# Two recurrent mixers of a decoder layer: post stages taken in turn, and 64-row products issued in pairs

## The chip, the cores and the metric

The kernel runs on one core of a Trainium2 chip. The metric is the device time of one execution in microseconds. The kernel before was timed three times; the median is 2287.77 us (2284.74 to 2293.57).

## The reference

Two decoder layers work on 512 tokens of width 1024 in float32. Each layer adds three sub-layers to x, each between two RMS norms:

```python
ff = swiglu(rms_norm(x, g0), w1, w3, w2);  x = x + 0.5 * rms_norm(ff, g1)      # FFN A, 1024 -> 2816 -> 1024
p  = rms_norm(x, g2) @ w_in                                                    # one projection for three mixers
y_a = rwkv7_time_mix(...)    # 4 heads x 64, delta-rule state, scan over tokens
y_b = s5_mix(...)            # complex diagonal state space
y_c = gated_deltanet_mix(...)# 4 heads x 128, chunked delta rule
x = x + rms_norm(concat(y_a, y_b, y_c) @ w_out, g3)
ff = swiglu(rms_norm(x, g4), ...);         x = x + 0.5 * rms_norm(ff, g5)      # FFN B
```

RWKV's step is `S = S*w + (S nkk) b + v k` and `y = S r` for every token. GDN carries a state from chunk to chunk in the same manner. Both are computed here in chunks of 128 tokens: products inside a chunk give triangular matrices, which are inverted, and then the state goes through the chunks one after the other.

## The kernel before

The 512 tokens are two halves of 256; a half is two chunks (c = 0, 1) of 128. The program is a list of stages, a letter, the layer and the half: `A00 a01 P00 M00 A01 o00 P01 r01 O00 g01 M01 B00 O01 ...`, and the same for layer 1, which ends `g11 M11 B10 O11 b10 B11`. A and B are the FFNs, P the projection, M the mixers, O the output projection. A stage M has much small work, and so the FFN of the other half is written behind it: A01 behind M00, B00 behind M01, A11 behind M10, B10 behind M11. Instructions that are written earlier have the higher rank, and a planner with a cost model sets each engine's order when the program is built. On the chip each engine keeps that order and waits where an operand isn't there yet.

All weights are float32. ScalarE splits each tile into a rounded high part (`whi`, line 226) and VectorE makes the low part (`wlo`, line 227); a product is three matmuls (lines 245 to 247), named `ph` (FFN up), `acc` (FFN down and output projection), `pp` and `pg`. The small products of the mixers are plain float32 matmuls, each of which the trace shows as two instructions.

RWKV's chunk products (lines 754 to 777, in `rwkv`). The four heads lie in pairs j = 0, 1 on 128 partitions; a head of 64 rows is the lower (o = 0) or the upper half (o = 1) of them. For each chunk c and each o, two products over 64 rows (j = 0, 1) go to a PSUM tile `pk` (line 760), VectorE masks it into `AK` (line 761); two more go to a PSUM tile `pb` (line 764), and VectorE makes `AT` (line 767, twice) and `AB` (line 769) of it. Behind both o stand the products `pav` (line 774) and their copies `RV` and `YV`. `mx` is the PSUM tag of all the mixers' small products; it has two buffers of one bank each.

The post stages (`rwkv_post`, line 780; `gdn_post`, line 962) carry the states. `mix` calls rwkv_post(0), gdn_post(0), rwkv_post(1), gdn_post(1). Each is a chain in which TensorE and VectorE (with ScalarE and GpSimd at the norms) take turns: rwkv_post from line 791 to the copy into `mixT` at line 852; gdn_post from line 976 to the copy at line 1033. `mixT` is what stage O multiplies by w_out (lines 1349 to 1356). GDN's SBUF tiles and many others share the tag `b2` with 12 buffers, RWKV's have the tag `b1` with 7.

Of the kernel before, what the change touches and what calls it, by code (L numbers as in the profile page):

```python
# [16 lines left out]
AF = mybir.ActivationFunctionType  # L17
ALU = mybir.AluOpType
AX = mybir.AxisListType

P = 128
# [20 lines left out]
class Trunk:  # L42
# [601 lines left out]
    def rwkv(self, l, h, I):  # L644
        nc, L = self.nc, self.L
# [45 lines left out]
        be = self.b2([P, 2, 2, P], "be")  # L691
# [50 lines left out]
        for src, dst, sc in ((be, bn, -1.0), (ka, kn, 1.0), (vv, vn, 1.0)):  # L742
            pt = self.mx([P, 2, 2, P], "ptn")
            m = 2 if h == 0 or src is vv else 1
            for c in range(m):
                for j in range(2):
                    nc.tensor.transpose(pt[:, c, j], src[:, j, c], self.ident)
            nc.scalar.activation(dst[:, 0:m].rearrange("p c (j k) -> p c j k", j=2), pt[:, 0:m], AF.Copy, scale=sc)

        AT = self.b4([P, 8, P], "AT")  # L750
        AB = self.b4([P, 8, P], "AB")
# [1 line left out]
        YV = self.b2([P, 2, 256], "YV")  # L753
        for c in range(2):
            AK = self.b4([P, 2, 2, 2, P], "AK")
            for o in range(2):
                q = slice(64 * o, 64 * o + 64)
                pk = self.mx([P, 2, 2, P], "pk")
                for j in range(2):
                    nc.tensor.matmul(pk[:, j], ka[q, j, c], ar[q, j, c], start=True, stop=True)  # L760
                nc.vector.tensor_tensor(AK[:, :, o], pk, self.maskK.unsqueeze(1).to_broadcast([P, 2, 2, P]), ALU.mult)
                pb = self.mx([P, 2, 2, P], "pb")
                for j in range(2):
                    nc.tensor.matmul(pb[:, j], be[q, j, c], ar[q, j, c], start=True, stop=True)
                for j in range(2):
                    hd = 2 * j + o
                    nc.vector.scalar_tensor_tensor(AT[:, 4 * c + hd], pb[:, j, 0], rn2[:, c, hd:hd + 1], self.maskB[:, 0],
                                                   ALU.mult, ALU.mult)
                nc.vector.tensor_tensor(AB[:, 4 * c:4 * c + 4].rearrange("p (j o) t -> p j o t", o=2)[:, :, o], pb[:, :, 1],
                                        self.maskB[:, 1:2].to_broadcast([P, 2, P]), ALU.mult)  # L770
            pv = self.mx([P, 2, 256], "pav")
            for z in range(2):
                for hd in range(4):
                    nc.tensor.matmul(pv[:, z, 64 * hd:64 * hd + 64], AK[:, hd // 2, hd % 2, z], vn[:, c, 64 * hd:64 * hd + 64],
                                     start=True, stop=True)
            nc.vector.tensor_copy(RV[:, c], pv[:, 0])
            nc.scalar.activation(YV[:, c], pv[:, 1], AF.Copy)
        yield dict(AT=AT, AB=AB, ar=ar, RV=RV, YV=YV, kn=kn, bn=bn, vn=vn, rn2=rn2, sb=sb, gref=gref, gend=gend, sg=sg)

    def rwkv_post(self, l, h, c, R_, W, mixT):  # L780
# [4 lines left out]
        if not first:  # L785
            S0 = self.b1([P, 2, P], "S0")
            for j in range(2):
                nc.vector.tensor_scalar(S0[:, j], self.Sr[:, j], gref[:, j, c:c + 1], None, ALU.mult)
            p1 = self.mx([P, 256], "p1")
            for j in range(2):  # L790
                nc.tensor.matmul(p1[:, j * P:(j + 1) * P], ar[:, j, c, 0], S0[:, j], start=True, stop=True)
            R = self.b1([P, 256], "R")
            nc.vector.tensor_tensor(R, p1, RV[:, c], ALU.add)
        else:
            R = RV[:, c]
        p2 = self.mx([P, 256], "p2")
        for hd in range(4):
            nc.tensor.matmul(p2[:, 64 * hd:64 * hd + 64], W[:, 4 * c + hd], R[:, 64 * hd:64 * hd + 64], start=True, stop=True)
        SA = self.b1([P, 256], "SA")
        nc.vector.tensor_tensor(SA.rearrange("p (h k) -> p h k", h=4), p2.rearrange("p (h k) -> p h k", h=4),  # L800
                                rn2[:, c].unsqueeze(2).to_broadcast([P, 4, 64]), ALU.mult)
        if not last:
            p3 = self.mx([P, 2, P], "p3")
            for j in range(2):
                s = slice(j * P, (j + 1) * P)
                nc.tensor.matmul(p3[:, j], kn[:, c, s], vn[:, c, s], start=True, stop=False)
                nc.tensor.matmul(p3[:, j], bn[:, c, s], SA[:, s], start=False, stop=True)
            Sn = self.lay.tile([P, 2, P], F32, tag="Sr", name=self.n("Sr"), bufs=2)
            if first:
                t = p3  # L810
            else:
                t = self.b1([P, 2, P], "St")
                nc.vector.tensor_tensor(t, p3, S0, ALU.add)
            bdm = self.hmask
            for j in range(2):
                nc.vector.scalar_tensor_tensor(Sn[:, j], t[:, j], gend[:, j, c:c + 1], bdm, ALU.mult, ALU.mult)
            self.Sr = Sn
        p4 = self.mx([P, 256], "p4")
        for j in range(2):
            if not first:  # L820
# [4 lines left out]
                                 start=first, stop=first or o == 1)  # L825
        y = self.b1([P, 4, 64], "y")
        nc.vector.tensor_tensor(y, p4.rearrange("p (h k) -> p h k", h=4), YV[:, c].rearrange("p (h k) -> p h k", h=4), ALU.add)

        bc = lambda t: t.unsqueeze(2).to_broadcast([P, 4, 64])
        s1 = self.sm([P, 4], "gs1")  # L830
# [15 lines left out]
        pg = self.mx([P, 256], "pg")  # L846
        nc.tensor.matmul(pg, sg[:, c * P:(c + 1) * P], L["wg2"], start=True, stop=True)
        nc.vector.tensor_tensor(yf, yf, pg, ALU.mult)
        pt = self.mx([P, 2, P], "pty")
        for j in range(2):  # L850
            nc.tensor.transpose(pt[:, j], yf[:, j * P:(j + 1) * P], self.ident)
# [111 lines left out]
    def gdn_post(self, l, h, c, I, G_, W, mixT):  # L963
# [9 lines left out]
        for src, dst, sc in ((lambda hd: v2[:, hd, tk], vs, sk), (lambda hd: qk[:, hd, 0, tk], kd, kds))[:1 if last else 2]:  # L973
            pt = self.mx([P, 4, P], "ptg")
            for hd in range(4):
                nc.tensor.transpose(pt[:, hd], src(hd), self.ident)
            nc.vector.tensor_tensor(dst, pt, bch(sc[:, h4]), ALU.mult)
        if not first:
            S = self.Sg
            p1 = self.mx([P, 4, P], "g1")  # L980
            for hd in range(4):
                nc.tensor.matmul(p1[:, hd], qk[:, hd, 0, tk], S[:, hd], start=True, stop=True)
            R = self.b2([P, 4, P], "Rg")
            for hd in range(4):
                nc.vector.scalar_tensor_tensor(R[:, hd], p1[:, hd], neg[:, 4 * c + hd:4 * c + hd + 1], vs[:, hd],
                                               ALU.mult, ALU.add)
            if not last:
                Sd = self.b2([P, 4, P], "Sd")
                nc.vector.tensor_tensor(Sd, S, bch(eg[:, 1, h4]), ALU.mult)
        else:  # L990
            R = vs
        p2 = self.mx([P, 4, P], "g2")
# [1 line left out]
            nc.tensor.matmul(p2[:, hd], W[:, 4 * c + hd], R[:, hd], start=True, stop=True)  # L994
        vt = self.b2([P, 4, P], "vt")
        nc.vector.tensor_tensor(vt, p2, bch(es[:, h4]), ALU.mult)
        if not last:
            p5 = self.mx([P, 4, P], "g5")
            for hd in range(4):
                nc.tensor.matmul(p5[:, hd], kd[:, hd], vt[:, hd], start=True, stop=True)  # L1000
            Sn = self.lay.tile([P, 4, P], F32, tag="Sg", name=self.n("Sg"), bufs=2)
            if first:
                nc.scalar.activation(Sn, p5, AF.Copy)
            else:
                nc.vector.tensor_tensor(Sn, p5, Sd, ALU.add)
        o = self.b2([P, 4, P], "og")
        if not first:
            p3 = self.mx([P, 4, P], "g3")
            for hd in range(4):
                nc.tensor.matmul(p3[:, hd], qk[:, hd, 1, tk], S[:, hd], start=True, stop=True)  # L1010
            nc.vector.tensor_tensor(o, p3, bch(eg[:, 0, h4]), ALU.mult)
        p4 = self.mx([P, 4, P], "g4")
        for hd in range(4):
            nc.tensor.matmul(p4[:, hd], AQ[:, 4 * c + hd], vt[:, hd], start=True, stop=True)
# [1 line left out]
            nc.scalar.activation(o, p4, AF.Copy)  # L1016
        else:
            nc.vector.tensor_tensor(o, p4, o, ALU.add)
        if not last:
            self.Sg = Sn  # L1020
        osq = self.b2([P, 4, P], "osq")
        ss = self.sm([P, 4], "oss")
        for hd in range(4):
# [3 lines left out]
        nc.gpsimd.tensor_tensor(r, r, rqs[:, h4], ALU.mult)  # L1027
        for hd in range(4):
            nc.vector.scalar_tensor_tensor(o[:, hd], o[:, hd], r[:, hd:hd + 1], gw[:, c, hd * P:(hd + 1) * P], ALU.mult, ALU.mult)
        pt = self.mx([P, 4, P], "pto")  # L1030
        for hd in range(4):
            nc.tensor.transpose(pt[:, hd], o[:, hd], self.ident)
# [286 lines left out]
    def mix(self, l, h, I):  # L1319
        mixT = self.inp.tile([P, KT, HALF], F32, tag="mixT", name=self.n("mixT"))  # L1320
        if "R" not in I:
            I["R"] = self.rwkv(l, h, I)
            next(I["R"])
        R_ = next(I["R"])
        G_ = self.gdn(l, h, I)
        ATs = (R_["AT"], G_["AT"])
        X0 = self.inverse(ATs)
        self.s5(l, h, I, mixT)
        W = self.inverse2(ATs, X0)
        for c in range(2):  # L1330
            self.rwkv_post(l, h, c, R_, W[0], mixT)
            self.gdn_post(l, h, c, I, G_, W[1], mixT)
        return mixT

    def outmul(self, l, k, mixT, plain, chunks, accs):
# [153 lines left out]
```

## Time and profile before

| | us |
|---|---|
| median of three runs | 2287.77 |
| the profiled execution | 2288.75 |
| its span in the profile | 2287.0 |
| TensorE busy (15800 matmul instructions) | 2226.2, 97% |
| VectorE busy | 1688.1, 74% |
| ScalarE busy | 1192.6, 52% |
| GpSimd busy | 168.2, 7% |
| granted TensorE clock, mean | 0.989 |

Times in the rows below are us from the start of the span; "x" ahead of a number is a count. Matmuls overlap in the array, and so what one costs is read from start to start, not from its duration.

### The profile page before, as it was taken

The page shows a single profiled execution, that of the slowest core. Times are in us where ns is not written, and L with a number is a line of the kernel's source. Part 1 is how long each engine was busy: PE and PEld are TensorE (multiplying, and loading weights), DVE is VectorE, ACT ScalarE, POOL GpSimd, SP SyncE. Part 2 cuts the span into 40 slices and gives each one's busy share as a digit, 9 for nine tenths or more (in the row PEclk, how much of TensorE's full clock was granted, in tenths as well). Part 3 has the DMA queues.
Part 4 walks back from the last instruction along what each step waited for, and adds up shares of the span by engine and source line. Part 5 has one row for each costly group of instructions (what it writes and reads, how often), then busy time and mean ns, then how long its engine had stood idle before and what let it go on. Part 6 is the DMA issues. An engine that isn't in the chain of part 4 may idle for free. (4 is left out here: it accounts for less than half of the span.)

```text
span 2287.0 us, 44455 instructions
## 1 busy us (share of the span) xinstructions
PE 2226.2 (97%) x15800; PEld 2043.2 (89%) x15800; DVE 1688.1 (74%) x3771; ACT 1192.6 (52%) x2521; POOL 168.2 (7%) x372
## 2 busy tenths in 40 slices
PE   8998999999999999999999999999999999998998
PEld 7998999997979999799899999889987889987997
DVE  6697886966877866859776688687687678667665
ACT  5555754544645544545555567445455445445554
POOL 2032000001100001202200010000020000001000
PEclk9999999999999999999999999999999899999999
DMA  6676764645765645576666677456467366445665
GB/s 200 197 210 189 182 189 138 202 141 175 192 184 169 188 137 151 172 204 205 205 178 188 187 195 193 140 181 176 141 192 217 105 184 170 137 137 179 190 187 156
DMA packets 604963, 403.67 MB, mean 177 GB/s; under 512 B 63306, under 2 KB 534340, under 8 KB 604740
## 3 DMA queue, kind: packets, MB, share of 16 engines
q1 hardware_dynamic: 604740, 400.82, 60.7%
q8 instruction: 124, 2.03, 0.4%
q14 instruction: 99, 0.81, 0.1%
HBM read 387.09 MB, written 13.63 MB: 175 GB/s over the span
## 5 line engine op out<-in xcount | busy, mean ns | idle before, releaser
L226 ACT ACTIVATE whi<-raw 128x512 fp32r<-128x512 f32 (+2 forms) x1296 | 813.0, 632 | 848.2 <-PE ph L246 418.6
L227 DVE TENSOR_TENSOR wlo<-raw,whi 128x512 fp32r<-128x512 f32 (+2 forms) x1296 | 888.6, 690 | 419.1 <-ACT whi L226 403.9
L247 PE MATMUL ph<-hth,wlo 128*128 128x256 f32 x2464 | 704.7, 286 | 5.2 <-DVE wlo L227 5.2
L245 PE MATMUL ph<-hth,whi 128*128 128x256 f32 x2464 | 701.3, 285 | 6.6 <-DVE gu L364 3.4
L246 PE MATMUL ph<-htl,whi 128*128 128x256 f32 x2464 | 701.9, 285 | 3.3 <-DVE htl L318 3.0
L245 PEld LDWEIGHTS ph<-hth,whi 128*128 128x128 f32 x2464 | 467.7, 190 | 19.4 <-issue 3.9
L246 PEld LDWEIGHTS ph<-htl,whi 128*128 128x128 f32 x2464 | 466.9, 190 | 16.5 <-DVE htl L318 4.5
L247 PEld LDWEIGHTS ph<-hth,wlo 128*128 128x128 f32 x2464 | 467.5, 190 | 13.8 <-DVE wlo L227 8.6
L246 PE MATMUL acc<-wlo,gh 128*128 128x512 f32 x704 | 276.2, 397 | 0.0
L247 PE MATMUL acc<-whi,gl 128*128 128x512 f32 x704 | 270.3, 396 | 0.0
L245 PE MATMUL acc<-whi,gh 128*128 128x512 f32 x704 | 256.8, 400 | 0.7 <-ACT whi L226 0.7
L247 PEld LDWEIGHTS acc<-whi,gl 128*128 128x128 f32 x704 | 131.4, 188 | 28.5 <-issue 0.3
L246 PEld LDWEIGHTS acc<-wlo,gh 128*128 128x128 f32 x704 | 131.9, 188 | 23.2 <-issue 1.0
L245 PEld LDWEIGHTS acc<-whi,gh 128*128 128x128 f32 x704 | 130.2, 189 | 23.1 <-issue 1.4
L245 PE MATMUL pp<-hth,whi 128*128 128x256 f32 x352 | 99.1, 282 | 1.7 <-ACT whi L226 1.6
L245 PE MATMUL ph<-hx,whi 128*128 128x256 f32 x352 | 99.7, 283 | 0.9 <-DVE gu L364 0.9
L370 ACT ACTIVATE gh<-gu 128x256 fp32r<-128x256 f32 x176 | 71.7, 408 | 53.5 <-DVE gu L364 52.3
L246 PE MATMUL ph<-hx,whi 128*128 128x256 f32 x352 | 99.5, 283 | 0.0
L247 PE MATMUL ph<-hx,wlo 128*128 128x256 f32 x352 | 99.4, 282 | 0.0
L247 PE MATMUL pp<-hth,wlo 128*128 128x256 f32 x352 | 98.6, 282 | 0.5 <-DVE wlo L227 0.5
L246 PE MATMUL pp<-htl,whi 128*128 128x256 f32 x352 | 98.7, 282 | 0.0
L245 PE MATMUL pp<-hx,whi 128*128 128x256 f32 x352 | 98.6, 281 | 0.0
(491 smaller groups left out, 3391.8 us busy)
## 6 DMA issues: line engine op xcount, KB each, us to landing
raw<-in_ffn_w SPq DMA_DIRECT2D x1056, 256.0 KB
raw<-in_w_in SPq DMA_DIRECT2D x176, 256.0 KB
raw<-in_w_out SPq DMA_DIRECT2D x96, 256.0 KB
raw<-in_w_in SPq DMA_DIRECT2D x32, 260.0 KB
gain<-in_norm_gain SPq DMA_DIRECT2D x28, 256.0 KB
lx<-s5w SPq DMA_DIRECT2D x16, 384.0 KB
lv<-s5w SPq DMA_DIRECT2D x16, 256.0 KB
x<-in_x SPq DMA_DIRECT2D x4, 512.0 KB
```

Of the source, the lines that this page charges most:

```text
L226: nc.scalar.activation(hi, q, AF.Copy)
L227: nc.vector.tensor_tensor(lo, q, hi.bitcast(F32), ALU.subtract)
L245: mm(out, lh, rh, start=start, stop=False)
L246: mm(out, lh, rl, start=False, stop=False)
L247: mm(out, ll, rh, start=False, stop=stop)
L370: nc.scalar.activation(gh, u, AF.Copy, scale=0.5)
```

## The change

The four products of the two `pk` tiles of a chunk are issued as one sequence that alternates between upper and lower rows (o = 1, 0), one PSUM tile for each half; then the same for the two `pb` tiles. The first product of such a pair waits for what frees both tiles (`behind`), the others are kept in order by `after`, which adds no wait. For `pb` that is the second `AK` operation and a new one-column VectorE copy, `seen`, that reads its result. The post stages become generators that stop at `yield`; `mix` takes them in turn. When one says True, its state is done, and the same mixer's chunk 1 is put at the head of the list.

```diff
-            nc.scalar.activation(dst[:, 0:m]..., pt[:, 0:m], AF.Copy, scale=sc)
+            freed = [nc.scalar.activation(dst[:, 0:m]..., pt[:, 0:m], AF.Copy, scale=sc)]
...
         for c in range(2):
             AK = self.b4([P, 2, 2, 2, P], "AK")
+            def pair(name, a, behind):
+                ps = [self.mx([P, 2, 2, P], name) for _ in range(2)]
+                i = None
+                for j in range(2):
+                    for o in (1, 0):
+                        q = slice(64 * o, 64 * o + 64)
+                        m = nc.tensor.matmul(ps[o][:, j], a[q, j, c], ar[q, j, c], start=True, stop=True)
+                        if i is not None:
+                            self.after(m, i)
+                        else:
+                            for b in behind:
+                                self.tc.add_manual_dep(m.ins, b.ins.name, mybir.DependencyInfo(
+                                    mybir.DependencyClass.Sync, mybir.DependencyReason.SCHED_ONLY), reason="pair")
+                        i = m
+                return ps
+            pks = pair("pk", ka, freed)
             for o in range(2):
-                q = slice(64 * o, 64 * o + 64)
-                pk = self.mx([P, 2, 2, P], "pk")
-                for j in range(2):
-                    nc.tensor.matmul(pk[:, j], ka[q, j, c], ar[q, j, c], start=True, stop=True)
-                nc.vector.tensor_tensor(AK[:, :, o], pk, self.maskK..., ALU.mult)
-                pb = self.mx([P, 2, 2, P], "pb")
-                for j in range(2):
-                    nc.tensor.matmul(pb[:, j], be[q, j, c], ar[q, j, c], start=True, stop=True)
+                kept = nc.vector.tensor_tensor(AK[:, :, o], pks[o], self.maskK..., ALU.mult)
+            pbs = pair("pb", be, [kept, nc.vector.tensor_copy(self.sm([P, 1], "seen"), AK[:, 1, 1, 1, P - 1:])])
+            for o in range(2):
+                pb = pbs[o]
                 for j in range(2):          # AT and AB as before
...
-            nc.vector.tensor_copy(RV[:, c], pv[:, 0])
-            nc.scalar.activation(YV[:, c], pv[:, 1], AF.Copy)
+            freed = [nc.vector.tensor_copy(RV[:, c], pv[:, 0]), nc.scalar.activation(YV[:, c], pv[:, 1], AF.Copy)]
...
# rwkv_post: "yield" after R, SA, y and the gate product; "yield True" after the new state Sr
# gdn_post:  "yield" after each of vs and kd, R, vt, the first og, the second og, the normed og;
#            "yield True" after the new state Sg (self.Sg = Sn moves up there)
...
-        for c in range(2):
-            self.rwkv_post(l, h, c, R_, W[0], mixT)
-            self.gdn_post(l, h, c, I, G_, W[1], mixT)
+        live = [(self.rwkv_post(l, h, 0, R_, W[0], mixT), 0), (self.gdn_post(l, h, 0, I, G_, W[1], mixT), 1)]
+        while live:
+            for t in list(live):
+                said = next(t[0], False)
+                if said is False:
+                    live.remove(t)
+                elif said and t[1] < 2:
+                    live.insert(0, (self.gdn_post(l, h, 1, ...) if t[1] else self.rwkv_post(l, h, 1, ...), 2))
```

## Rows read from the trace of the kernel before

**Rows 1.** The page: engine, busy us, share of the span, instructions.
```profile
PE 2226.2 (97%) x15800; PEld 2043.2 (89%) x15800; DVE 1688.1 (74%) x3771; ACT 1192.6 (52%) x2521; POOL 168.2 (7%) x372
```
**Rows 2.** Waits of PE: line waited for, us in total, times, longest.
```profile
PE pto L1032 <- DVE og L1029: 2.5, 2, 2.0
```
**Rows 3.** Stage of the chunk products in M00: stretch, length, busy us by engine, PEclk, DMA share, GB/s.
```profile
326.80:360.80 34.00, 34.00 (x214) 28.31 (x212) 22.27 (x54) 12.48 (x24) 0.00 (x0) 1.00 0.44 129
```
**Rows 4.** Timeline of PE, stage M00: start us, us, instruction.
```profile
336.57 0.28 PE L245 MATMUL ph<-hth,whi 128*128 128x256 f32 x1
336.79 1.13 PE L764 MATMUL pb<-ar,be 64*128 64x256 f32 x4
337.84 0.39 PE L246 MATMUL ph<-htl,whi 128*128 128x256 f32 x1
338.07 0.28 PE L247 MATMUL ph<-hth,wlo 128*128 128x256 f32 x1
338.19 0.28 PE L245 MATMUL ph<-hth,whi 128*128 128x256 f32 x1
```
**Rows 5.** Timeline of PE, stage M01, where two groups lie together.
```profile
678.42 0.28 PE L245 MATMUL ph<-hth,whi 128*128 128x256 f32 x1
678.62 0.48 PE L764 MATMUL pb<-ar,be 64*128 64x256 f32 x1
678.64 0.48 PE L760 MATMUL pk<-ar,ka 64*128 64x256 f32 x1
...
679.39 0.38 PE L760 MATMUL pk<-ar,ka 64*128 64x256 f32 x1
679.70 0.39 PE L246 MATMUL ph<-htl,whi 128*128 128x256 f32 x1
679.92 0.28 PE L247 MATMUL ph<-hth,wlo 128*128 128x256 f32 x1
```
**Rows 6.** Timeline of PE, stage M11.
```profile
1793.67 0.41 PE L245 MATMUL ph<-hth,whi 128*128 128x256 f32 x1
1794.01 2.07 PE L764 MATMUL pb<-ar,be 64*128 64x256 f32 x4
1796.02 0.58 PE L246 MATMUL ph<-htl,whi 128*128 128x256 f32 x1
1796.39 0.41 PE L247 MATMUL ph<-hth,wlo 128*128 128x256 f32 x1
```
**Rows 7.** Stretches of stage M11, columns as in rows 3.
```profile
1789.50:1806.60 17.10, 17.10 (x54) 12.56 (x54) 8.37 (x28) 4.01 (x8) 0.00 (x0) 0.50 0.06 16
2051.03:2055.76 4.73, 4.73 (x11) 3.76 (x12) 2.34 (x5) 2.10 (x4) 0.00 (x0) 0.50 0.49 154
```
**Rows 8.** Instructions on tile pk: duration ns min/median/max, first and last start.
```profile
L760 PE MATMUL pk<-ar,ka x64: 376/376/792, 333.4 to 1814.1; 64*128 64x256 f32 x64
L761 DVE TENSOR_TENSOR AK<-pk,maskK x16: 678/692/694, 334.6 to 1814.5; 128x512 f32<-128x512 f32 x16
```
**Rows 9.** Instructions on tile pb.
```profile
L764 PE MATMUL pb<-ar,be x64: 376/376/792, 336.8 to 1817.3; 64*128 64x256 f32 x64
L767 DVE SCALAR_TENSOR_TENSOR AT<-pb,rn,maskB x32: 335/343/351, 338.0 to 1818.0; 128x128 f32<-128x128 f32 x32
L769 DVE TENSOR_TENSOR AB<-pb,maskB x16: 406/412/416, 338.5 to 1818.3; 128x256 f32<-128x256 f32 x16
```
**Rows 10.** Timeline of PE, first product of M11's post stages.
```profile
1959.57 0.61 PE L791 MATMUL p<-S,ar 128*128 128x128 f32 x4
```
**Rows 11.** Instructions on tile mixT between 1950 and 2052 us.
```profile
L852 ACT ACTIVATE mixT<-pty x2: 384/384/385, 1983.6 to 2030.7; 128x256 f32<-128x256 f32 x2
L1033 ACT ACTIVATE mixT<-pto x2: 597/598/599, 2009.8 to 2050.4; 128x512 f32<-128x512 f32 x2
```
**Rows 12.** Timeline of PE at the end of M11's post stages.
```profile
2047.71 0.30 PE L1032 MATMUL pto<-ident,og 128*128 128x128 f32 x1 [2.00 <-DVE og L1029]
2051.03 0.79 PE L245 MATMUL acc<-whi,mh 128*128 128x512 f32 x1 [0.69 <-ACT mixT L1033]
```

More of the change, by code (lines that the diff above doesn't have):

```diff
@@ L747, in rwkv @@
                     nc.tensor.transpose(pt[:, c, j], src[:, j, c], self.ident)
-            nc.scalar.activation(dst[:, 0:m].rearrange("p c (j k) -> p c j k", j=2), pt[:, 0:m], AF.Copy, scale=sc)
+            freed = [nc.scalar.activation(dst[:, 0:m].rearrange("p c (j k) -> p c j k", j=2), pt[:, 0:m], AF.Copy, scale=sc)]
         AT = self.b4([P, 8, P], "AT")
@@ L755, in rwkv @@
             AK = self.b4([P, 2, 2, 2, P], "AK")
-            for o in range(2):
-                q = slice(64 * o, 64 * o + 64)
-                pk = self.mx([P, 2, 2, P], "pk")
-                for j in range(2):
-                    nc.tensor.matmul(pk[:, j], ka[q, j, c], ar[q, j, c], start=True, stop=True)
-                nc.vector.tensor_tensor(AK[:, :, o], pk, self.maskK.unsqueeze(1).to_broadcast([P, 2, 2, P]), ALU.mult)
-                pb = self.mx([P, 2, 2, P], "pb")
-                for j in range(2):
-                    nc.tensor.matmul(pb[:, j], be[q, j, c], ar[q, j, c], start=True, stop=True)
+            def pair(name, a, behind):
[14 more added lines that the diff above has]
+            pks = pair("pk", ka, freed)
+            for o in range(2):
+                kept = nc.vector.tensor_tensor(AK[:, :, o], pks[o], self.maskK.unsqueeze(1).to_broadcast([P, 2, 2, P]), ALU.mult)
+            pbs = pair("pb", be, [kept, nc.vector.tensor_copy(self.sm([P, 1], "seen"), AK[:, 1, 1, 1, P - 1:])])
+            for o in range(2):
+                pb = pbs[o]
                 for j in range(2):
@@ L793, in rwkv_post @@
             nc.vector.tensor_tensor(R, p1, RV[:, c], ALU.add)
+            yield
         else:
@@ L801, in rwkv_post @@
                                 rn2[:, c].unsqueeze(2).to_broadcast([P, 4, 64]), ALU.mult)
+        yield
         if not last:
@@ L817, in rwkv_post @@
             self.Sr = Sn
+        yield True
         p4 = self.mx([P, 256], "p4")
@@ L827, in rwkv_post @@
         nc.vector.tensor_tensor(y, p4.rearrange("p (h k) -> p h k", h=4), YV[:, c].rearrange("p (h k) -> p h k", h=4), ALU.add)
+        yield
         bc = lambda t: t.unsqueeze(2).to_broadcast([P, 4, 64])
@@ L848, in rwkv_post @@
         nc.vector.tensor_tensor(yf, yf, pg, ALU.mult)
+        yield
         pt = self.mx([P, 2, P], "pty")
@@ L977, in gdn_post @@
             nc.vector.tensor_tensor(dst, pt, bch(sc[:, h4]), ALU.mult)
+            yield
         if not first:
@@ L989, in gdn_post @@
                 nc.vector.tensor_tensor(Sd, S, bch(eg[:, 1, h4]), ALU.mult)
+            yield
         else:
@@ L996, in gdn_post @@
         nc.vector.tensor_tensor(vt, p2, bch(es[:, h4]), ALU.mult)
+        yield
         if not last:
@@ L1005, in gdn_post @@
                 nc.vector.tensor_tensor(Sn, p5, Sd, ALU.add)
+            self.Sg = Sn
+        yield True
         o = self.b2([P, 4, P], "og")
@@ L1011, in gdn_post @@
             nc.vector.tensor_tensor(o, p3, bch(eg[:, 0, h4]), ALU.mult)
+            yield
         p4 = self.mx([P, 4, P], "g4")
@@ L1018, in gdn_post @@
             nc.vector.tensor_tensor(o, p4, o, ALU.add)
-        if not last:
-            self.Sg = Sn
+        yield
         osq = self.b2([P, 4, P], "osq")
@@ L1029, in gdn_post @@
             nc.vector.scalar_tensor_tensor(o[:, hd], o[:, hd], r[:, hd:hd + 1], gw[:, c, hd * P:(hd + 1) * P], ALU.mult, ALU.mult)
+        yield
         pt = self.mx([P, 4, P], "pto")
@@ L1329, in mix @@
         W = self.inverse2(ATs, X0)
-        for c in range(2):
-            self.rwkv_post(l, h, c, R_, W[0], mixT)
-            self.gdn_post(l, h, c, I, G_, W[1], mixT)
+        live = [(self.rwkv_post(l, h, 0, R_, W[0], mixT), 0), (self.gdn_post(l, h, 0, I, G_, W[1], mixT), 1)]
[5 more added lines that the diff above has]
+                elif said and t[1] < 2:
+                    live.insert(0, (self.gdn_post(l, h, 1, I, G_, W[1], mixT) if t[1] else self.rwkv_post(l, h, 1, R_, W[0], mixT), 2))
         return mixT
```

## The prediction

> **What bounds the kernel now.** I read the page's table of engines first: TensorE is busy for 2226.2 of 2287.0 us, VectorE for 1688.1, ScalarE for 1192.6 [rows 1]. Then the list of TensorE's waits: at the post stages it has one line, the last transposes `pto` behind VectorE's `og`, twice, 2.5 us in all [rows 2]; no line there has a wait on `AK`, `AT` or `AB`. Then the stretches in which the chunk products run: in M00 TensorE is busy for all of 34.00 us, VectorE for 22.27, the DMA engines for 0.44 [rows 3]. So in these stages TensorE's order is full, the FFN of the other half lies between the small products, and an instruction that goes there is time that the stage gives back. Last the timeline around single products, since busy time hides what overlaps: a full FFN matmul `ph` starts 0.12 us behind the one before it, although it lasts 0.28 [rows 4].
>
> **Change 1, the 64-row products.** In each of the four stages M there are 2 chunks x 2 halves x 2 kinds = 8 groups, 32 in all; a group is two products, four instructions (64 + 64 instructions on `pk` and `pb` in the trace [rows 8, 9]). The price of a group is read from start to start over its neighbours: from 336.57 to 338.07 is 1.50 us, in which two `ph` steps of 0.12 stand, so 1.26 us: 1.05 for the four instructions, 0.20 for going from `ph` to them and back [rows 4].
>
> What two groups cost when they lie together the trace before already shows once. In M01 a `pb` group of the lower rows met a `pk` group of the upper rows: their instructions start 0.02 us apart (678.62 and 678.64), all eight have started by 679.39, and from 678.42 to 679.92 is again 1.50 us [rows 5]. So eight instructions on both halves cost the same 1.26 us as four on one. That is the pattern that the change makes on purpose, with two PSUM tiles as there.
>
> The clock was not the same in all stages. From 1789.50 to 1806.60 the granted clock was 0.50 of full speed, which is 1.2 GHz [rows 7]; a group there costs 1796.39 - 1793.67 = 2.72 us less two `ph` steps of 0.215, so 2.29 us [rows 6]. Four of M11's groups fall into it, the other 28 run at 2.4 GHz, two of these together. Before: 27 x 1.26 + 4 x 2.29 = 43.2 us. After, 16 pairs: 14 x 1.26 + 2 x 2.29 = 22.2 us. TensorE saves 21.0 us.
>
> Bounds: if the halves did not overlap, a pair would cost 2 x 1.05 + 0.20 = 2.30 instead of 2.52, and 16 x 0.2 = 3 us would be left (the change of neighbours alone). If each change between lower and upper rows cost as much as one half of the way from `ph` and back, 0.10, three such changes in a pair take 16 x 0.3 = 5 us, and 2 us would be lost. So 2 us lost to 21.0 saved; I take 21.0, because the row nearest to it is the same two instructions on the same operands [rows 5]. It goes to the end undiminished: TensorE is full there [rows 3], and what it finds earlier is the FFN that would run next.
>
> **What the pairs add.** The first product of a pair now waits for both tiles, and everything behind it on TensorE's order waits too. For `pb` that is two `AK` operations of 0.692 us and the copy `seen` (its price has no row; nothing to 0.34, the time of an `AT` operation on 128 columns, and I take a little over half) [rows 8, 9]: 1.4 to 1.7 us of VectorE that have to be filled with some 12 to 15 `ph` matmuls of 0.12. Before, every group waited in the same way for a tile that VectorE or ScalarE frees, and the order kept them apart: 3.4 us lie between the first `pk` (333.4 [rows 8]) and the first `pb` (336.8 [rows 9]), filled with `ph` (the last of them stands in [rows 4]), and TensorE did not wait. I expect the same planner to fill the new distance, and enter 2.0 us for misses; the bounds are 0 and the uncovered waits (second rival). The eight `seen` copies, 8 x 0.34 = 2.7 us at most, lie in VectorE's idle third [rows 3].
>
> The Trainium skill (Perfetto Trace Analysis, section Matmuls) speaks against this part: independent groups of matmuls should rotate through PSUM banks, so that the evacuation of one overlaps the matmuls of the next, and a pair takes both banks at once. Here the overlap comes from `ph`, which has banks of its own, and the trace agrees as far as no wait on `AK` or `AB` stands in the list [rows 2]; by that rule without such cover the second rival would hold.
>
> **Change 2, the post stages in turn.** No instruction goes and none is added; no DMA is in it. In M11 the stages run from 1959.57 to 2050.98 [rows 10, 11], 91.4 us, strictly one mixer behind the other: RWKV chunk 0 lands in mixT at 1983.6, GDN at 2009.8, RWKV chunk 1 at 2030.7, GDN at 2050.4 [rows 11], so about 24, 26, 21 and 20 us. Each chain mostly waits on itself, and RWKV and GDN share nothing but engines, the two `mx` buffers and the rings of SBUF tiles. Taken in turn, two chains of GDN are the longer sum, 26 + 20 = 46 us at least; I take 50 to 60. What is that worth? Not 35 us, as TensorE was full all the while with FFN B10. It is worth what TensorE lost at the end, when that cover was used up: 2.00 us for `og` and 0.69 for mixT [rows 12], and the half clock that followed, 4.73 us at 0.50, of which half is lost, 2.4 [rows 7]; in M01 the other 0.5 of the 2.5 us [rows 2]. Sum 5.6 us. Since change 1 shortens the cover in M11 by some 7 us more (four groups at either clock become two), the old order would have given part of the 21.0 back at this place; with the post 30 us shorter it doesn't.
>
> M00 and M10 gain nothing by it: their chunk 1 is covered by the next projection. The steps are moved past each other on TensorE's, VectorE's, ScalarE's and GpSimd's orders. TensorE's price can move: a product between two `ph` costs 0.20 us for its neighbours, there are (6 + 8) x 2 x 4 = 112 products in the post stages, and if a quarter find other neighbours that is 28 x 0.2 = 5.6 us either way. I take nothing. GpSimd's few norm operations and SP's queue have no part in it.
>
> **Sum.** 2288.75 - 21.0 - 5.6 + 2.0 = 2264.2 us for the profiled execution. The median of the runs shown is 1.0 below that execution, so I forecast **2263 us**. Its own range: without the misses and with 5.6 us won on neighbours, 2255.6; with 5.6 lost and no tail won, 2274.4.
>
> **The rivals.**
>
> *The post stages give something back.* Two RWKV and two GDN chains in flight need more tiles of the rings (seven `b1` tiles of 7 for one RWKV post; seven `b2` tiles of 12 for one GDN post, beside five of `b2` that RWKV keeps), so a tile of chunk 1 waits for one of chunk 0, and chunk 0, which stage o00 wants first, is delayed by chunk 1, which is put ahead of it. For it: the rings are full on paper. Against it: 91.4 us had to shrink by only some 10 for the tail to go. Price: no tail won, 8 us lost at o00 and O01, 2288.75 - 21.0 + 2.0 + 8 - 1.0 = 2277 (2270 to 2280).
>
> *Slower: the pair's head is uncovered.* If the planner places a pair where too little `ph` is ready, TensorE stands for the evacuation: 8 x (2 x 0.692 + 0.34) = 13.8 us ahead of `pb`, and 2.20 us (`AT` twice and `AB`, for both halves: 4 x 0.343 + 2 x 0.412 [rows 9]) 8 times behind it, 17.6 us; 31.4 against 21.0 saved, so 2288.75 + 10.4 - 1.0 = 2298. It decides from 1.3 us a pair on. If the clock then falls in the other three stages as in M11, 17.10 us at half each, 25.6 us more: 2324. For it: M11's stretch at 0.50, in which only two or three `ph` stood between groups [rows 6, 7]. Against it: not one of the 32 groups had such a wait.
>
> *The change doesn't do what it says.* The order is laid down, that the products lie side by side is not; if others come between, or if alternating does not overlap, 3 us remain of change 1: 2288.75 - 3 - 5.6 + 2 - 1.0 = 2281. Against it: [rows 5].
>
> *More than forecast.* M11's half clock lasts 17.10 us because little dense work lies between its groups; with two groups fewer the dense stretch comes 4.6 us earlier, and some 2 us more at 2.4 GHz are won, with all else at its best: 2250 to 2255.
>
> **Chances.** Forecast 0.66; more 0.06; post gives back 0.14 (half of it under 2276.3); no overlap 0.08; uncovered heads 0.06. A measurement can tell 0.5%, 11.4 us, from no change: under 2276.3 is faster, over 2299.2 slower. Faster 0.66 + 0.06 + 0.07 + 0.01 = 0.80; same 0.07 + 0.07 = 0.14; slower 0.06. The range 2254 to 2279 leaves out the slow cases, the most of no overlap, and the best end.
>
> **What would show it.** Eight 64-row instructions in each of 16 places, starting 0.02 us apart in twos and done in 1.1 us; no row of TensorE waiting on `AK`, `seen`, `RV` or `YV` of any size; post stages of 50 to 60 us in M01 and M11, with mixT complete before B00 and B10 run out, and no wait on `og`; the clock at 1.00 where it fell at 2049. It is wrong if the two halves start 0.2 us or more apart, if pairs open with idle TensorE of over 1 us, or if the time saved comes back as idle TensorE in front of O or P.

## The result and the profile after

The changed kernel takes 2262.14 us (median of 6 runs, 2257.09 to 2267.37) against 2286.26 us for the kernel before beside it; the ratio is 0.9891, 95% interval 0.9866 to 0.9916. Run once more with the experiments it was 2262.81 us, ratio 0.9887 (0.9863 to 0.9910). The forecast was 2263 us. The sum was right; where the time came from was not, as the stages below and the next two sections show.

The page of the changed kernel, busy time by engine:

```profile
PE 2204.1 (97%) x15800; PEld 2032.1 (90%) x15800; DVE 1688.2 (75%) x3779; ACT 1191.7 (53%) x2521; POOL 163.2 (7%) x372
```

Against [rows 1] the instructions are the same but for eight on VectorE, the `seen` copies; TensorE is busy for 22.1 us less in a span that is 26.0 us shorter. So most of the gain is time in which TensorE works, as was expected, and its waits changed little in sum. Not all of it is overlap, though: what runs at the half clock is busy for longer, and the granted clock of these two executions is 0.989 and 0.992.

Timeline of TensorE in M00, a pair:

```profile
333.63 0.28 PE L247 MATMUL ph<-hth,wlo 128*128 128x256 f32 x1
333.83 1.13 PE L763 MATMUL pk<-ar,ka 64*128 64x256 f32 x8
334.90 0.39 PE L245 MATMUL ph<-hth,whi 128*128 128x256 f32 x1
335.12 0.28 PE L246 MATMUL ph<-htl,whi 128*128 128x256 f32 x1
```

From 333.63 to 335.12 is 1.49 us for eight instructions, where [rows 4] had 1.50 for four. In all 16 pairs the eight instructions stand side by side and begin within 0.76 us.

Instructions of line 776, the new copy:

```profile
L776 DVE COPY seen<-AK x8: 143/144/150, 336.2 to 1803.2; 128x1 f32<-128x1 f32 x8
```

Two of TensorE's waits, the longest of stage O and the only one at the head of a pair; `pto` is not in the list any more ([rows 2] had 2.5 us):

```profile
PE acc L1386 <- DVE x L341: 2.2, 1, 2.2
PE pk L763 <- ACT vn L748: 0.2, 1, 0.2
```

M11's post stages: the first product, then the copies into mixT between 1930 and 2052 us:

```profile
1949.21 0.61 PE L804 MATMUL p<-S,ar 128*128 128x128 f32 x4
```
```profile
L870 ACT ACTIVATE mixT<-pty x2: 372/378/384, 1981.1 to 2003.2; 128x256 f32<-128x256 f32 x2
L1057 ACT ACTIVATE mixT<-pto x2: 599/600/600, 2003.6 to 2015.7; 128x512 f32<-128x512 f32 x2
```

They last from 1949.21 to 2016.3, 67 us, where [rows 10, 11] had 91.4. The last copy now comes some 38 us before TensorE next stands idle (2054). The clock at M11's start and over its end:

```profile
1782.70:1786.10 3.40, 3.40 (x15) 3.11 (x15) 3.26 (x12) 2.21 (x7) 0.00 (x0) 0.52 0.00 0
1786.10:1817.00 30.90, 30.51 (x228) 27.16 (x227) 22.37 (x60) 12.75 (x28) 0.00 (x0) 1.00 0.38 112
2000.00:2054.00 54.00, 54.00 (x318) 47.50 (x317) 38.18 (x71) 31.66 (x71) 4.67 (x10) 1.00 0.58 179
```

(Stretch, length, busy us of PE, PEld, DVE, ACT, POOL, each with its number of instructions, then the granted clock, the DMA engines' share and GB/s.) The half clock lasts 3.4 us instead of the 17.10 of [rows 7], and the one at the end of the stage is gone; TensorE is full from 2000 to 2054.

To see by stage where the time went, take the first `pw` product of each stage M as a mark (here of the changed kernel):

```profile
305.53 0.48 PE L658 MATMUL pw<-th,wa 64*128 64x256 f32 x1
637.25 0.48 PE L658 MATMUL pw<-th,wa 64*128 64x256 f32 x1
1414.37 0.48 PE L658 MATMUL pw<-th,wa 64*128 64x256 f32 x1
1751.31 0.48 PE L658 MATMUL pw<-th,wa 64*128 64x256 f32 x1
```

The same marks in three profiles of the kernel before and two of the changed one give these means (us between marks):

| stretch | before | after | difference | forecast |
|---|---|---|---|---|
| start to M00 | 309.6 | 307.0 | -2.6 | 0 |
| M00, A01, o00, P01 | 332.8 | 330.5 | -2.3 | -5.0 |
| M01, B00, O01, A10 and on | 775.9 | 776.9 | +1.0 | -4.3 |
| M10, A11, o10, P11 | 340.4 | 337.2 | -3.2 | -5.0 |
| M11 to the end | 527.6 | 509.5 | -18.1 | -12.2 |

(Forecast: pairs and tails as the prediction prices them, without its 2.0 us for misses. The first stretch holds nothing that changed; its 2.6 us is what such means can differ by. Two of the three profiles before have the long half clock in M11, 530.0 and 531.8 us to the end, and the third, with 3.4 us of it, has 520.9.)

### The profile page after: what moved, and what is told of

Same layout as the page of the kernel before. It is cut to its first block, busy times and chain, and to the rows that moved or that the text cites. A ratio compares the mean times of both kernels' runs of the same rounds, so it can differ in the third digit from the quotient of the medians.

```text
span 2261.0 us, 44455 instructions
## 1 busy us (share of the span) xinstructions
PE 2204.1 (97%) x15800; PEld 2032.1 (90%) x15800; DVE 1688.2 (75%) x3779; ACT 1191.7 (53%) x2521; POOL 163.2 (7%) x372
## 4 chain that ended last, share of the span: by engine, by line
PE 87%; DVE 5%; DMA 4%; issue 1%; ACT 1%; POOL 0%; SPq 0%; DVEq 0%; ACTq 0%; POOLq 0%
PE ph L247 14%; PE ph L246 14%; PE ph L245 14%; PE acc L245 7%; PE acc L246 7%; PE acc L247 7%; PE pp L245 4%; PE pp L247 4%; PE pp L246 4%; PE acc L1386 2%; DVE wlo L227 1%; PE xt L309 1%; DMA blk<-scr 1%; PE py L610 1%; DMA raw<-in_w_in 1%
```

## The experiments

Times are medians; each ratio is to the kernel before, timed beside it. The kernel before took 2286.92 us beside the first, second and fourth row, 2290.13 beside the fifth, sixth and eighth, 2289.53 beside the seventh.

| kernel | us | ratio | 95% |
|---|---|---|---|
| pairs alone | 2280.57 | 0.9983 | 0.9965 to 1.0 |
| post stages alone | 2277.77 | 0.9956 | 0.9937 to 0.9976 |
| both (the change) | 2262.14 | 0.9891 | 0.9866 to 0.9916 |
| both, no alternation | 2269.37 | 0.9932 | 0.9913 to 0.9952 |
| post, pairs in M00 and M10 | 2269.13 | 0.9916 | 0.9884 to 0.9947 |
| post, pairs in M01 and M11 | 2275.37 | 0.9932 | 0.9909 to 0.9954 |
| post, pairs in all but M01 | 2260.67 | 0.9872 | 0.9848 to 0.9895 |
| both, chunk 0 ranked first | 2261.85 | 0.9884 | 0.9854 to 0.9913 |

**Pairs alone.**

```diff
-        live = [...]; while live: ...
+        for c in range(2):
+            for _ in self.rwkv_post(l, h, c, R_, W[0], mixT):
+                pass
+            for _ in self.gdn_post(l, h, c, I, G_, W[1], mixT):
+                pass
```

> The 64-row products in pairs as in the changed kernel, the post stages in the old order. Theory (the overlap of the two halves is the gain, the post order saves only the tail of M11): about 2268 us, some 19 us under before and 5.6 over the changed kernel; the wait on og and the half clock at about 2045 us are back. Rival (the post order brings the gain): about 2281 us. Rival (the gain is M11's clock): 2265 to 2272, and nearly all of it won in M11 with the half clock of 17 us at its start gone.

It was 2280.57 us. That is the number of the first rival, but not for its reason, since the post order alone does not bring the gain either (next run); the theory and the other rival were wrong. 21 us of saved TensorE time made 4 (0 to 8; 6 between the medians). The waits on `pto` say where it went, first the sum, then the two places, M01 and M11:

```profile
PE pto L1056 <- DVE og L1052: 8.8, 2, 4.5
```
```profile
918.89 0.45 PE L1056 MATMUL pto<-ident,og 128*128 128x128 f32 x1 [4.33 <-DVE og L1052]
...
2036.80 0.44 PE L1056 MATMUL pto<-ident,og 128*128 128x128 f32 x1 [4.50 <-DVE og L1052]
2041.14 0.79 PE L245 MATMUL acc<-whi,mh 128*128 128x512 f32 x1 [0.69 <-ACT mixT L1057]
```

In M01 TensorE's other work is through at 914.6, 0.6 us later than before, but the post chain ends later still: its last transposes start at 918.89, where before they started at 914.52:

```profile
914.52 0.30 PE L1032 MATMUL pto<-ident,og 128*128 128x128 f32 x1 [0.52 <-DVE og L1029]
```

The wait grows from 0.52 to 4.33 us. In M11 TensorE is through 13 us earlier and the chain only 11 (both are helped by this profile's short half clock at the start of M11, 3.4 us), so the wait grows from 2.00 [rows 12] to 4.50 us, with a longer half clock behind it:

```profile
2034.40:2044.60 10.20, 7.11 (x18) 5.38 (x19) 4.06 (x9) 3.72 (x7) 1.60 (x4) 0.50 0.18 53
```

10.20 us at 0.50, where before it was 6.8, which costs half of the difference, 1.7. So 6.3 us of waits on `og` and 1.7 of clock are 8 of the 17 us that did not arrive; the other 9 have no single place. A full engine is the bound only as long as the chain beside it has slack; in M11 both ended together, and a lighter TensorE met the chain. Why the chain itself came later in M01 no run shows.

**Post stages alone.** The changed kernel with the loop over `o` of the kernel before (lines 756 to 770) in the place of the pairs.

> The post stages in turn as in the changed kernel, the 64-row products in the old order. Theory: before less the tail of M11, 2280 to 2283 us, and the half clock of about 17 us at the start of M11 is there as before, since the single 64-row groups are back. Rival (the post order brings the gain): about 2265 us. Rival (M11's clock goes by chance or by what stands ahead of it): under 2275, with M11's half clock gone although the groups are single.

2277.77 us, 10 us under before (5 to 14), somewhat more than the theory's 4 to 7. The end of M11 is as in the changed kernel, the start is as in the kernel before:

```profile
1788.50:1805.60 17.10, 16.84 (x53) 12.17 (x52) 8.86 (x30) 4.54 (x12) 0.00 (x0) 0.50 0.06 16
2000.00:2070.00 70.00, 70.00 (x435) 62.63 (x435) 50.26 (x96) 40.50 (x93) 8.08 (x16) 1.00 0.58 171
```

Alone the two parts give 4 and 10 us, together 25: they are not additive. M11 shows why, if profiles with the same half clock at its start, 3.4 us, are compared, from M11's mark to the end: before 520.9 us, with pairs alone 520.9, with the post order and single groups 515.0 (the run with pairs in M00 and M10, below), one profile each; with the post order and pairs 510.0, the mean of five. So the pairs are worth nothing there in the old post order and 5.0 us in the new one, which brings the slack that they spend.

**No alternation.**

```diff
-                for j in range(2):
-                    for o in (1, 0):
+                for o in (1, 0):
+                    for j in range(2):
```

> The changed kernel, but a pair's four products are issued upper, upper, lower, lower instead of upper, lower, upper, lower; waits, tiles and all else are the same. If TensorE overlaps only what is next in its order: 12 to 17 us slower than the changed kernel (a pair takes 2.1 us instead of 1.06, 16 times), 2274 to 2279 us. If lower and upper rows overlap wherever they lie in one sequence: no difference, 2262 us.

2269.37 us lies between the two. 12 of the 16 pairs still stand whole and start in twos 0.01 us apart, and one takes 1.07 us to the next `ph`: the halves overlap wherever they lie in one sequence. The other four were torn apart by the planner. One of each kind in M00:

```profile
333.98 1.14 PE L763 MATMUL pk<-ar,ka 64*128 64x256 f32 x8
335.05 0.39 PE L245 MATMUL ph<-hth,whi 128*128 128x256 f32 x1
```

```profile
338.89 0.28 PE L247 MATMUL ph<-hth,wlo 128*128 128x256 f32 x1
339.10 1.13 PE L763 MATMUL pb<-ar,be 64*128 64x256 f32 x4
340.16 0.38 PE L245 MATMUL ph<-hth,whi 128*128 128x256 f32 x1
340.47 1.13 PE L763 MATMUL pb<-ar,be 64*128 64x256 f32 x4
341.53 0.38 PE L246 MATMUL ph<-htl,whi 128*128 128x256 f32 x1
```

Four torn pairs at 1.26 us are an estimated 5 of the 7 us between the medians. Alternation serves to keep a pair whole, not to make it overlap.

**The kernel before again**, twice, for its profile.

> The kernel before, unchanged, for a second profile. If M11's half clock of 17 us comes from its single 64-row groups, it is there again, 14 to 20 us long, at about 1790 us. If it was chance of that one execution, it is under 7 us or elsewhere, and the time is about 2279 us.

> The kernel before, for a third profile. So far the half clock at the start of M11 lasted 17.1 us in one of its two profiles. If single 64-row groups bring it about now and then, 17 us are as likely as 3.4 here; if it needs something else, 3.4.

The half clock at M11's start in each of the two; in the first also what followed:

```profile
1791.60:1795.00 3.40, 3.32 (x13) 2.77 (x14) 3.27 (x14) 2.14 (x7) 0.00 (x0) 0.50 0.00 0
1795.00:1812.00 17.00, 17.00 (x101) 13.48 (x102) 11.21 (x34) 5.40 (x11) 0.00 (x0) 1.00 0.22 63
```
```profile
1791.00:1808.10 17.10, 17.09 (x54) 12.75 (x55) 8.30 (x30) 4.01 (x8) 0.00 (x0) 0.50 0.06 17
```

3.4 us in the one (2283.78 us), 17.10 in the other (2291.32 us).

**The post stages alone again.**

> The kernel with the post stages alone, for a second profile: single groups in M11, no wait on og at the end. As for the kernel before: 17 us or 3.4 us of half clock at the start of M11; the run with 17 us is the slower one by about 7 us.

```profile
1791.60:1808.70 17.10, 16.77 (x50) 12.20 (x51) 9.61 (x34) 4.96 (x12) 0.00 (x0) 0.50 0.06 16
```

17.10 again, now at 2283.43 us, where the first run had 2278.31 with the same 17.1: there is no pair to show the expected 7 us. All kernels of this document together have 13 profiles. With single groups in M11 the half clock at its start lasted 17.1 us in 4 of 6; with pairs in M11 it lasted 3.4 us in 7 of 7 (in one of these, without alternation, half of M11's pairs were torn). In every one the clock fell within 4 us ahead of M11's first `pk` product. That the single groups have a part in the long half clock is thus likely, not certain: something else is needed too, as the two of 3.4 us show. It is not how long ahead of that product the clock fell, 3.2 and 3.3 us in these two, 1.1 to 3.5 us in the four. What it is stays open.

**Pairs in one half of the sequence.** `if h == 0:` (or `h == 1`) around the new code, the old code in the else branch; post stages in turn in both.

> Post stages in turn everywhere; 64-row products in pairs in M00 and M10 alone, in the old order in M01 and M11. Theory (each stage's TensorE saving goes to the end where the cover lasts, less what the waits there take): 8 pairs save 10.1 us against the kernel with the post stages alone (2277.8 us), less some 3 us: 2269 to 2271 us. Rival (only M11 pays, the other stages give their lead back to VectorE and to loads): 2275 to 2278 us. Single groups are back in M11, so the half clock of 17 us at its start can come back.

> The counterpart: pairs in M01 and M11 alone, old order in M00 and M10, post stages in turn everywhere. Theory: 3.8 us in M01 and 5 to 9 in M11 (by the clock there) against the kernel with the post stages alone (2277.8 us): 2265 to 2269 us. Rival (M01's saving is lost where stage O01 waits for w_out): 2269 to 2272 us. In either case no half clock over 7 us at the start of M11, and the savings of this and of the counterpart together make some 15.6 us, the difference of the changed kernel from the kernel with the post stages alone.

2269.13 us for M00 and M10 is the theory's; 2275.37 for M01 and M11 is above both ranges, though by no more than the kernel before was slower here (2290.13 against 2286.92). By the ratios their pairs are worth only some 5.5 us (0.9932 against 0.9956), those of M00 and M10 some 9.1 (0.9916). Together that is 14.6, and between the post stages alone and the changed kernel lie 14.9 (0.9956 against 0.9891). Each ratio has an interval of some 5 to 7 us to either side, so that these sums agree better than they can be known; but the marks below say the same: given the new post order, the stages add up.

**Pairs in all but M01.** The condition is `h == 0 or l == 1`.

> The changed kernel, but with the 64-row products of M01 alone in the old order. Theory (M01's pairs bring nothing: what TensorE saves there, 3.8 us, comes back as waits for the prenorm's tiles in the chunk stage and behind FFN B00): within 2 us of the changed kernel run beside it. Rival (M01's saving goes to the end like that of M00): 3 to 5 us slower than the changed kernel.

> The changed kernel, unchanged, beside the others: 2259 to 2265 us. At the start of M11 a half clock of 3.4 us, not 17.

2260.67 against 2262.81 us beside it: not slower, so M01's pairs bring nothing. The stretch from M01's mark to M10's says so too, 776.6 us in the mean of four profiles with pairs in M01 and 774.9 in four without, all in the new post order. In the changed kernel TensorE waits in M01's chunk stage for the prenorm's tiles, which the kernel without pairs there doesn't do:

```profile
664.93 0.38 PE L245 MATMUL ph<-hth,whi 128*128 128x256 f32 x1 [0.33 <-ACT hth L317]
...
668.78 0.38 PE L246 MATMUL ph<-htl,whi 128*128 128x256 f32 x1 [0.92 <-DVE htl L318]
```

That is 1.25 us of the 3.8 (which the pairs of M01 should have saved); for the rest the runs name no single place. The intervals overlap (0.9848 to 0.9895 and 0.9863 to 0.9910), so this is no proof of a faster version.

**Chunk 0 ranked first.** `live.append(...)` for `live.insert(0, ...)`.

> The changed kernel, but chunk 1 of a mixer is put at the end of the list instead of its head, so that chunk 0 has the higher rank. Theory (TensorE is full while the post stages run, and only their end counts): within 3 us of the changed kernel, 2260 to 2265 us, with the first transposes of pto in M00 4 us or more earlier than its 545.7. Rival (stages o00 and o10 lose time because chunk 0 now lands 11 us later than before): 3 to 6 us faster, 2256 to 2259 us.

2261.85 us, as the theory had it. `pto` of M00 comes 5.7 us earlier (the first row; the second is the changed kernel) and nothing follows from it:

```profile
539.95 0.49 PE L1056 MATMUL pto<-ident,og 128*128 128x128 f32 x3
```
```profile
545.68 0.60 PE L1056 MATMUL pto<-ident,og 128*128 128x128 f32 x4
```

## Why the prediction was right in its sum, and where not

**The price of a pair** was right: 1.49 us where [rows 5] gave 1.50; all 16 begin within 0.76 us, and none was torn apart or paid for its changes of rows. The rival of no overlap is out.

**"It goes to the end undiminished" is a step that failed, in M00 and M01.** It was read from a stretch that is full before [rows 3]. In M00, M01 and M10 the pairs and M01's tail were to give 14.3 us; the marks show 4.5. The marks of the other kernels part the pairs from the post order. All of these have the post stages in turn, and the number of profiles is in brackets (the run without alternation is left out; for M11 only profiles with 3.4 us of half clock at its start):

| stretch | single groups | pairs | saved | forecast |
|---|---|---|---|---|
| from M00 | 332.7 (3) | 329.3 (5) | 3.4 | 5.0 |
| from M01 | 774.9 (4) | 776.6 (4) | -1.7 | 3.8 |
| from M10 | 343.2 (3) | 337.2 (5) | 6.0 | 5.0 |
| from M11 | 515.0 (1) | 510.0 (5) | 5.0 | 5.0 at 2.4 GHz |

So the saving of the pairs goes to the end whole in M10 and M11, a part of it is lost in M00, and in M01 all of it. M00 shows how: TensorE gets ahead of the FFN's weights, and at the inversion, where VectorE is busy for 45.86 of 50 us, it waits for a low part and then for a load of S5. Before, VectorE was as busy there (the first row; the second is the changed kernel), but TensorE stood still for 0.21 us, where it now does for 2.37:

```profile
400.00:450.00 50.00, 49.79 (x353) 46.18 (x353) 47.61 (x112) 25.02 (x46) 0.24 (x2) 1.00 0.69 204
400.00:450.00 50.00, 47.63 (x338) 44.83 (x337) 45.86 (x107) 22.98 (x42) 0.23 (x2) 0.97 0.66 195
```
```profile
404.40 0.38 PE L247 MATMUL ph<-hth,wlo 128*128 128x256 f32 x1 [1.57 <-DVE wlo L227]
...
425.02 0.43 PE L1313 MATMUL y<-U,lx 128*128 128x64 f32 x2 [0.80 <-DMA lx<-s5w]
```

The wait on `wlo` is there, 0.7 to 1.6 us long, in all seven profiles of kernels with pairs in M00 and in none of those without. So the next bound, a VectorE over nine tenths busy 50 us behind the pairs, took part of the lead. Where M01's went is open. (The 0.97 is a half clock of 3.4 us behind these waits; of the seven profiles only this one has it.) The 2.0 us entered for misses were looked for at the heads of the pairs, where the trace has 0.2.

**The post stages** were right in kind and mis-sized: 67 us, not 50 to 60, and enough. The tail of M11 went whole: 2.69 us of waits and the half clock behind them. The prediction said that the old order "would have given part of the 21.0 back"; the pairs alone show that with the loss in the other stages it was 17 of 21. The Trainium skill (Perfetto Trace Analysis, section Matmuls) asks for groups that rotate through PSUM banks. The changed kernel, whose pairs each take both banks of their tag, has 0.2 us of waits at the heads of the pairs, since FFN products fill the distance. With the pairs alone the post chain of M01 ends 4.4 us later; whether the two banks that a pair holds are the cause no run shows.

**"M00 and M10 gain nothing by it", with a price taken as nothing,** held in M00 (332.4 us with the post order alone, 332.8 before) and not in M10. From M10's mark to M11's it was 340.0 to 340.6 us in three profiles before, and it is 342.8 and 343.6 in the two of the post order alone: 2.8 us are lost. The two marks before, then with the post order alone:

```profile
1416.37 0.48 PE L658 MATMUL pw<-th,wa 64*128 64x256 f32 x1
1757.02 0.48 PE L658 MATMUL pw<-th,wa 64*128 64x256 f32 x1
```
```profile
1415.26 0.48 PE L658 MATMUL pw<-th,wa 64*128 64x256 f32 x1
1758.01 0.48 PE L658 MATMUL pw<-th,wa 64*128 64x256 f32 x1
```

A part of it stands at the projection P11, where TensorE waits for tiles of the prenorm and did not before:

```profile
1688.75 0.39 PE L245 MATMUL pp<-hth,whi 128*128 128x256 f32 x1 [0.45 <-ACT hth L317]
1689.59 0.38 PE L246 MATMUL pp<-htl,whi 128*128 128x256 f32 x1 [0.46 <-DVE htl L318]
```

So M10's 3.2 us in the table of the result are pairs that gave all that was forecast and a post order that took some of it back.

**The clock** was the term that was too small, and by luck it made good what the other stages lost. The prediction took 4 of M11's groups at half clock as given, and 2.4 us at the tail. Over runs timed together the mean granted clock was 0.990 before, 0.990 with pairs alone and 0.993 with the post order alone; in the changed kernel's runs it was 0.994, and 0.993 when it was timed again. Of 2287 us a clock of 0.990 loses 23, one of 0.994 loses 14: so up to 9 us of the 25 are clock, an estimate, as the half clock costs nothing where TensorE waits. They come with the post order (no tail) and, by the 13 profiles, with the pairs at M11's start. M11's 18.1 us hold the 2.69 us of waits, the overlap of its pairs, and that clock.

**The rivals.** That the post stages give something back, with 0.14, came in a small part, as 2.8 us in M10; its form, chunk 0 delayed at o00, is out, as chunk 0 earlier by 5.7 us changed nothing, and the tail of M11 was won. Whether the rings of tiles have a part in M10's loss no run shows. The uncovered head, 0.06, did not come. "More than forecast" had the right place, with 2 us; a half clock of 3.4 us instead of 17.1 is worth 6.9, in the executions that have it. The reason that it gave, little dense work between the groups, isn't shown: the second profile of the kernel before has the same order and 3.4 us. (The 0.44 that the prediction reads beside the busy times of M00 [rows 3] is the share of the DMA engines, not us.)

## What to carry to other kernels

Here a stage that was full on one engine handed on what that engine saved only where the chain beside it and the engine behind it had slack; ask for both, and for the next 50 us too, not just for the stretch itself. Where two bounds end together, price an edit to each alone and then both: here 4 and 10 us made 25. A total that comes out right is no proof of its terms; marks at fixed instructions over several profiles of each kernel show it cheaply.

## What the runs showed of the hardware

Products over 64 rows on the lower and the upper half overlap, 0.01 us apart, also when four instructions of the one half stand in TensorE's order ahead of the four of the other (12 of 16 pairs without alternation, 1.07 us for eight). And where M11 began with single 64-row products, the granted clock stayed at 0.50 for 17.1 us in 4 of 6 profiles, though TensorE was busy for 16.8 to 17.1 us of it; where it began with pairs, the clock was back at 1.00 after 3.4 us in 7 of 7.
